# FFN-down of a transformer layer on one core: more 2x2 seven-product panels, with one weight sum formed by transfers

## The chip, the core and the metric

The kernel runs on one core of one Trainium2 chip. The core has five engines with a queue each: PE (TensorE, matrix products; the trace shows its weight loads apart, as PEld), DVE (VectorE), ACT (ScalarE), POOL (GpSimd) and SP (SyncE, which here only issues transfers). Each takes its instructions in order, and semaphores tie the queues together. The metric is the device time of one execution in microseconds (us); of several runs the median is given.

## What is computed

One layer for 256 tokens of width 2048, in float32: RMS norm, an input projection, a pooling mixer and an RWKV-7 mixer, the output projection, then the part that the change touches, and at the end a gate with per-layer embeddings and a final norm:

```python
h2 = rms_norm(x, mlp_norm[i])
x = x + jnp.square(jax.nn.relu(h2 @ w_ffn_up[i])) @ w_ffn_down[i]      # 2048 -> 8192 -> 2048

gate = jax.nn.sigmoid(rms_norm(x, ple_norm[i]) @ w_ple_gate[i])
x = x + gate * (p[i] @ w_ple_proj[i])
```

## The kernel before

**Products.** Each float32 product is made as three products of parts: a value is split into a rounded high part h and the rest l, and h·h, h·l and l·h are summed. A weight panel arrives raw in SBUF (`load_raw`, L149: transfers of 512 KB issued by SP; three buffers with the tag raw and three with raw2). ACT casts it to the high part (wh, two instructions of 512 columns), DVE subtracts to get the low part (wl = raw − wh, one instruction of 1024 columns). Then PE multiplies.

**Stages.** FFN-up and FFN-down run in two halves of 4096 hidden columns. A half is `ffn_half`: eight blocks f of FFN-up (`gemm_wide`; names u00, u01, u10 ... stand for block and half, with four loads each), which leave the activations y, split in h and l; then two sweeps of FFN-down, `down_sweep(hf, pair)`, one for the left and one for the right 1024 output columns. The sweeps are called d00, d01, d10 and d11 (half, then pair). The page and the trace leave numbers out of the names: d_b and d_w are PSUM banks of a sweep, raw_d its raw panels.

**A sweep** runs over 16 panels kp. Each panel is a 256 x 1024 piece of w_ffn_down, taken as a 2x2 of blocks w11, w12, w21, w22 of 128 x 512, against a 2x2 of activation blocks a11 ... a22. A *plain* panel takes the eight block products, each as three matmuls: 24 matmuls. A *square* (in the tuple `SEVEN`) takes seven products (the scheme of Strassen and Winograd): 21 matmuls. For this DVE forms four sums of weight blocks, t1 to t4 (L1269 to L1272), and in FFN-up the sums S of activations (`activation_sums`). Before, there are 7, 7, 7 and 4 squares in d00, d01, d10 and d11.

**Buffers.** In a square of before the halves are 'wa' (w11, its own tag), b (w21, w22), c (w1, w3) and d (w2, w4), in a plain panel a (w11, w12) and b (w21, w22). `halves_of` (L1233) takes them from three pairs with the tags wh and wl, which all stages share, and d from two buffers with the tag graw, which the kept gate weights (`keep`, called in d11 and in the gate's products) use too. The weight sums lie in a8(1, ...), one slot of the large buffers, each 128x2048. One buffer with the tag junk takes the squares of the norms' statistics (`rms_stat`, L298) and the activation sums on their way.

**What sets the order.** The program is written panel by panel, and a scheduler puts each engine's instructions in an order by priority: splits, weight sums and the adds at a sweep's end stand in `tc.high_priority` blocks, and so move ahead of other work as soon as their buffers allow. Buffers of a tag are handed out in the order of the program. At the end of a sweep's last square, the banks of products 1, 5, 6 and 7 are added into x (`add`, L1249), scaled by s2; those of the other four follow at the sweep's end.

## Time and profile before

| | us |
|---|---|
| runs | 1180.05, 1181.89, 1939.81 |
| median of the three | 1181.89 |
| the profiled execution | 1180.25 |
| its span in the trace | 1178.2 |
| first half of FFN-up | about 378 to 558 |
| sweeps d00, d01 | about 558 to 720 |
| second half of FFN-up | about 720 to 902 |
| sweeps d10, d11 | about 902 to 1070 |
| projection, gate, final norm | about 1070 to 1178 |

The span runs from the first to the last instruction of the profiled execution; 2.05 us lie outside it. One of the three runs took 1939.81 us; the other two differ by 0.16%. In the profile's rows, a row of the timeline has the start, the duration, engine, line and operation, the tile written and those read, and in brackets the idle time ahead of it with what ended it. PE's matmuls overlap one another, so their pace is read from start to start. PE's granted clock is 1.00 in all the stages of the table but the last (0.97).

### The profile page before, as it was taken

What the parts mean: (1) busy time and instruction counts of PE and PEld (TensorE: products, weight loads), DVE (VectorE), ACT (ScalarE), POOL (GpSimd) and SP (SyncE); (2) the same over time, 40 slices, a digit from 0 to 9 for tenths busy, and PEclk for the clock granted to TensorE, in tenths of its full rate; (3) what the DMA queues carried; (4) which work ended last, traced back from release to release, by engine and by line L of the source; (5) the groups of instructions that cost most, each with busy time, mean ns of one, the idle gap of its engine ahead of it and who ended that gap; (6) DMA issues with size and microseconds to landing.
All of it is one profiled execution on the core that took longest, in us unless ns stands there. A gap on an engine that the chain in (4) does not pass through costs nothing.

```text
span 1178.2 us, 17287 instructions
## 1 busy us (share of the span) xinstructions
PE 1162.5 (99%) x6419; PEld 973.4 (83%) x6419; DVE 873.3 (74%) x1188; ACT 709.3 (60%) x1309; POOL 13.7 (1%) x73
## 2 busy tenths in 40 slices
PE   8999999999999999999999999999999999999997
PEld 8787777788887888888888888888888888888886
DVE  7786996964656666767988987676668879788543
ACT  7776848676545565555665664555556655568543
POOL 2100000000000000000000000000000000000000
PEclk9999999999999999999999999999999999999999
DMA  7464343354465555555556556555555555767511
GB/s 290 154 202 146 135 140 119 119 179 157 160 203 178 177 182 196 184 192 200 187 204 212 198 202 209 186 191 191 185 195 190 202 205 195 290 233 249 197 56 72
DMA packets 60756, 216.81 MB, mean 184 GB/s; under 512 B 6784, under 2 KB 7552, under 8 KB 60288
## 3 DMA queue, kind: packets, MB, share of 16 engines
q1 hardware_dynamic: 60240, 214.99, 52.5%
q8 instruction: 50, 0.82, 0.3%
q10 hardware_dynamic: 432, 0.73, 0.2%
q14 instruction: 34, 0.28, 0.1%
HBM read 213.59 MB, written 2.10 MB: 183 GB/s over the span
## 4 chain that ended last, share of the span: by engine, by line
PE 96%; ACT 1%; DVE 1%; DMA 0%; issue 0%; SPq 0%; POOL 0%; DVEq 0%; POOLq 0%
PE u_w L1112 20%; PE u_w L1117 10%; PE d_b L1231 7%; PE d_b L1229 7%; PE d_b L1230 7%; PE d_w L1231 2%; PE d_w L1229 2%; PE d_w L1230 2%; PE gt_b L242 2%; PE gt_b L241 2%; PE gt_b L238 2%; PE zk_b L241 1%; PE zk_b L242 1%; PE o_b L241 1%; PE o_b L242 1%; PE zv_b L238 1%
## 5 line engine op out<-in xcount | busy, mean ns | idle before, releaser
L1112 PE MATMUL u_w<-h,wh_u 128*128 128x512 f32 x1024 | 321.9, 395 | 0.0
L167 ACT ACTIVATE wh_u<-raw_u 128x512 fp32r<-128x512 f32 x256 | 147.5, 623 | 160.9 <-issue 98.2
L168 DVE TENSOR_TENSOR wl_u<-raw_u,wh_u 128x1024 fp32r<-128x1024 f32 x128 | 156.6, 1224 | 105.2 <-ACT wh_u L167 103.5
L1117 PEld LDWEIGHTS u_w<-h,wl_u 128*128 128x128 f32 x1024 | 192.4, 188 | 45.4
L1117 PE MATMUL u_w<-h,wl_u 128*128 128x256 f32 x1024 | 201.4, 278 | 0.0
L1112 PEld LDWEIGHTS u_w<-h,wh_u 128*128 128x128 f32 x1024 | 156.0, 189 | 0.1
L168 DVE TENSOR_TENSOR wl_gt<-raw_gt,wh_gt 128x1024 fp32r<-128x1024 f32 x24 | 29.4, 1224 | 23.2 <-ACT wh_gt L167 23.2
L167 ACT ACTIVATE wh_gt<-raw_gt 128x512 fp32r<-128x512 f32 x48 | 28.0, 638 | 23.1 <-PE gt_b L242 14.4
L241 PE MATMUL gt_b<-wh_gt,h 128*128 128x512 f32 x96 | 37.3, 389 | 0.0
L242 PE MATMUL gt_b<-wh_gt,h 128*128 128x512 f32 x96 | 37.3, 389 | 0.0
L168 DVE TENSOR_TENSOR wl_o<-raw_o,wh_o 128x1024 fp32r<-128x1024 f32 x16 | 19.6, 1222 | 12.9 <-ACT wh_o L167 9.9
L167 ACT ACTIVATE wh_o<-raw_o 128x512 fp32r<-128x512 f32 x32 | 18.4, 623 | 16.3 <-issue 8.5
L167 ACT ACTIVATE wh_zp<-raw_zp 128x512 fp32r<-128x512 f32 x32 | 18.6, 623 | 15.7 <-PE zp_b L242 7.2
L168 DVE TENSOR_TENSOR wl_zk<-raw_zk,wh_zk 128x1024 fp32r<-128x1024 f32 x16 | 19.4, 1220 | 10.4 <-ACT wh_zk L167 10.4
L241 PE MATMUL zk_b<-wh_zk,hTh 128*128 128x512 f32 x64 | 25.2, 394 | 1.4 <-ACT wh_zk L167 1.4
L241 PE MATMUL zv_b<-wh_zv,hTh 128*128 128x512 f32 x64 | 26.0, 406 | 0.0
L167 ACT ACTIVATE wh_zk<-raw_zk 128x512 fp32r<-128x512 f32 x32 | 18.4, 622 | 12.4 <-PE zv_b L242 4.0
L241 PE MATMUL zp_b<-wh_zp,hTh 128*128 128x512 f32 x64 | 25.7, 401 | 0.0
L238 PE MATMUL gt_b<-wl_gt,h 128*128 128x512 f32 x96 | 25.7, 389 | 0.0
L168 DVE TENSOR_TENSOR wl_zv<-raw_zv,wh_zv 128x1024 fp32r<-128x1024 f32 x16 | 19.4, 1218 | 8.2 <-ACT wh_zv L167 7.4
L241 PE MATMUL zr_b<-wh_zr,hTh 128*128 128x512 f32 x64 | 25.4, 397 | 0.0
L242 PE MATMUL zp_b<-wh_zp,hTl 128*128 128x512 f32 x64 | 25.0, 391 | 0.0
(840 smaller groups left out, 2963.9 us busy)
## 6 DMA issues: line engine op xcount, KB each, us to landing
raw_u<-in_w_ffn_up_dram SPq DMA_DIRECT2D x128, 512.0 KB, 3.5
raw_d<-in_w_ffn_down_dram SPq DMA_DIRECT2D x128, 512.0 KB, 4.3
raw_gt<-in_w_ple_gate_dram SPq DMA_DIRECT2D x24, 512.0 KB, 3.5
raw_zk<-in_w_in_dram SPq DMA_DIRECT2D x16, 512.0 KB, 3.7
raw_zr<-in_w_in_dram SPq DMA_DIRECT2D x16, 512.0 KB, 3.3
raw_zv<-in_w_in_dram SPq DMA_DIRECT2D x16, 512.0 KB, 3.3
raw_zp<-in_w_in_dram SPq DMA_DIRECT2D x16, 512.0 KB, 3.2
raw_o<-in_w_out_dram SPq DMA_DIRECT2D x16, 512.0 KB, 4.2
```

Of the source, the lines that this page charges most:

```text
L167: nc.scalar.activation(wh[:, a * 512 : (a + 1) * 512], raw[:, a * 512 : (a + 1) * 512], AF.Copy)
L168: nc.vector.tensor_tensor(wl, raw, wh.bitcast(F32), op=ALU.subtract)
L238: nc.tensor.matmul(banks[tt], ah[:, ts_], halves[a][1], start=False, stop=last)
L241: nc.tensor.matmul(banks[tt], ah[:, ts_], halves[a][0], start=i + a == 0, stop=False)
L242: nc.tensor.matmul(banks[tt], al[:, ts_], halves[a][0], start=False, stop=False)
L1112: nc.tensor.matmul(bank[:, ct, :].rearrange("p (s t) -> p s t", s=2), wh[:, cs[ct]], hl, start=k == 0, stop=False, skip_group_check=True,)
L1117: nc.tensor.matmul(bank[:, ct, 0:T], wl[:, cs[ct]], hl[:, 0, :], start=False, stop=k == 15, skip_group_check=True)
L1229: nc.tensor.matmul(banks[n], ah, wh, start=first, stop=False)
L1230: nc.tensor.matmul(banks[n], ah, wl, start=False, stop=False)
L1231: nc.tensor.matmul(banks[n], al, wh, start=False, stop=last)
```

## The change

The layout of w_ffn_down on the host changes, so that a panel's four blocks can be loaded in other groupings. Per square three things change. First, SP loads rx = [w21 | w11] (512 KB) and ry = w22 alone (256 KB). Second, w12 goes into a slot of a *ring* of two slots (one 128x1024 buffer with the tag S) by a transfer that POOL issues, and a second transfer from POOL adds w11 to it on the way, so p1 = w11 + w12 comes without an engine. `begin_sum` issues both; it is called twice in FFN-up (f = 3 and 4), and then after each square, for the square two further on. Third, of the weight sums DVE forms t2 = p1 − w22 in place in the ring, and t43, the two sums for the pair d, in place in rx, with one instruction. w2 is split into a buffer with the tag junk; the tag wa is gone.

There are 9, 9, 9 and 5 squares now; in d00, d01 and d10 mostly two squares follow a plain panel. The half buffers of all panels come from four pairs in turn (three with the tags wh and wl, every fourth pair a pair of its own, wh4 and wl4); graw serves the kept gate weights and the ninth square's activation sums. One activation sum changes its sign, and two adds take ns2 = −s2. The squares of the norm n2 use the tag S ahead of the ring. The order of the panels in d01 changes.

```diff
-                junk = fp.tile([128, 1024], F32, tag="junk", bufs=1, name=f"junk_{name}{tt}{hf}")
+                junk = fp.tile([128, 1024], F32, tag="S" if name == "n2" else "junk", bufs=1, name=f"junk_{name}{tt}{hf}")
...
+        nc.vector.tensor_scalar_mul(ns2, s2, -1.0)
...
-    SEVEN = (1, 3, 5, 7, 9, 11, 13)
-    s_slots = (0, 2, 5)
+    SEVEN = (1, 3, 4, 6, 7, 9, 10, 12, 13)
+    s_slots = (0, 2, 5, 1)
+    ns2 = const.tile([128, 2], F32, name="ns2")
...
-        nc.vector.tensor_tensor(s3, a11, a21, op=ALU.subtract)
+        nc.vector.tensor_tensor(s3, a21, a11, op=ALU.subtract)
...
+    ring = []
+    squares_of = {}
+    visits_of = {}
+    for hf in range(2):
+        for pair in range(2):
+            last = hf + pair == 2
+            squares_of[hf, pair] = (1, 3, 6, 9, 12) if last else SEVEN
+            visits_of[hf, pair] = (0, 2, 1, 4, 3, *range(5, 16)) if last else (range(16), (0, 2, 1, 5, 3, 4, 8, 6, 7, 11, 9, 10, 14, 12, 13, 15))[pair]
+    in_line = [(*hp, kp) for hp, visits in visits_of.items() for kp in visits if kp in squares_of[hp]]
+    begun = []
+    turns = []
+
+    def slot(n):
+        return ring[0][:, n % 2 * 512 : n % 2 * 512 + 512]
+
+    def begin_sum():
+
+        n = len(begun)
+        if not ring:
+            ring.append(fp.tile([128, 1024], F32, tag="S", name="ring"))
+        if n < len(in_line):
+            hf, pair, kp = in_line[n]
+            nc.gpsimd.dma_start(slot(n), w_down[pair, hf * 16 + kp, 1, :, 1, :])
+            nc.gpsimd.dma_start(slot(n), w_down[pair, hf * 16 + kp, 0, :, 1, :], accum_op=ALU.add)
+            begun.append(n)
+
+    def summed(*square):
+        return slot(in_line.index(square))
+
+    def down_sweep(hf, pair, ys, sboxes, hooks=(), between=None):
 
         nm = f"d{hf}{pair}"
+        seven, visits = squares_of[hf, pair], visits_of[hf, pair]
...
-        def halves_of(src, name, own=False):
-
-            pool, kw = (fp, dict(bufs=2)) if own else (wp, {})
-            wh = pool.tile([128, 1024], F32R, tag="graw" if own else "wh", name=f"wh_{name}", **kw)
-            wl = pool.tile([128, 1024], F32R, tag="graw" if own else "wl", name=f"wl_{name}", **kw)
+        def half_tiles(name):
+
+            turns.append(name)
+            if len(turns) % 4 == 0:
+                return [fp.tile([128, 1024], F32R, tag=f"{hl}4", name=f"{hl}_{name}") for hl in ("wh", "wl")]
+            return [wp.tile([128, 1024], F32R, tag=hl, name=f"{hl}_{name}") for hl in ("wh", "wl")]
+
+        def halves_of(src, name):
+
+            wh, wl = half_tiles(name)
...
-        for q, kp in enumerate(((0, 2, 1, 4, 3, *range(5, 16)) if hf else (0, 2, 1, 4, 3, 6, 5, 8, 7, 10, 9, 12, 11, 14, 13, 15)) if pair else range(16)):
+        def add(tt, c, src, scale=s2):
+            nc.vector.scalar_tensor_tensor(xs(tt, c), src, scale[:, tt : tt + 1], xs(tt, c), op0=ALU.mult, op1=ALU.add)
+
+        def panel(kp, c, name, rows):
+
+            return load_raw(w_down[pair, hf * 16 + kp, c, :, 0:rows].rearrange("p r n -> p (r n)"), rows * 512, name)
+
+        for q, kp in enumerate(visits):
             if q in hooks:
                 hooks[q]()
             y, j = ys[kp // 2], kp % 2 * 512
             a11, a21, a12, a22 = ((y[:, j + i * 128 : j + i * 128 + 128], y[:, 1024 + j + i * 128 : 1152 + j + i * 128]) for i in range(4))
-            rx, ry = (load_raw(w_down[pair, hf * 32 + 2 * kp + i], 1024, f"{nm}_{kp}_{i}") for i in range(2))
+            rx, ry = (panel(kp, c, f"{nm}_{kp}_{c}", 1 if c and kp in seven else 2) for c in range(2))
             if kp in seven:
-                i = SEVEN.index(kp)
-                st = sboxes[kp][:, i % 2 * 1024 : i % 2 * 1024 + 1024]
+                st = s_of(sboxes, kp)
                 s1, s2_, s3, s4 = ((st[:, c * 128 : c * 128 + 128], st[:, 512 + c * 128 : 640 + c * 128]) for c in range(4))
-                t_ = a8(1, f"t{nm}_{kp}")
-                t1, t3, t2, t4 = (t_[:, c * 512 : c * 512 + 512] for c in range(4))
-                wa = fp.tile([128, 1024], F32R, tag="wa", name=f"wa{nm}_{kp}")
-                w11 = wa[:, 0:512], wa[:, 512:1024]
+                p1 = summed(hf, pair, kp)
+                t2 = p1
+                wa = fp.tile([128, 1024], F32R, tag="junk", bufs=1, name=f"wa{nm}_{kp}")
+                w2 = wa[:, 0:512], wa[:, 512:1024]
+                w21, w11 = halves_of(rx, f"{nm}_{kp}a")
+                wh, wl = half_tiles(f"{nm}_{kp}b")
+                w22, w1 = ((wh[:, c : c + 512], wl[:, c : c + 512]) for c in (0, 512))
                 with tc.high_priority(20000):
-                    split_sb(*w11, rx[:, 0:512])
-                w21, w22 = halves_of(ry, f"{nm}_{kp}b")
-                with tc.high_priority(20000):
-                    nc.vector.tensor_tensor(t1, rx[:, 512:1024], rx[:, 0:512], op=ALU.subtract)
-                    nc.vector.tensor_tensor(t3, ry[:, 512:1024], rx[:, 512:1024], op=ALU.subtract)
-                    nc.vector.tensor_tensor(t2, t3, rx[:, 0:512], op=ALU.add)
-                    nc.vector.tensor_tensor(t4, ry[:, 0:512], t2, op=ALU.subtract)
-                w1, w3 = halves_of(t_[:, 0:1024], f"{nm}_{kp}c")
-                w2, w4 = halves_of(t_[:, 1024:2048], f"{nm}_{kp}d", True)
-                for n, a_, w_ in (("1", a11, w11), ("2", a12, w21), ("3", s4, w22), ("5", s1, w1), ("7", s3, w3), ("6", s2_, w2), ("4", a22, w4)):
+                    split_sb(*w22, ry[:, 0:512])
+                    split_sb(*w1, p1)
+                    nc.vector.tensor_tensor(t2, p1, ry[:, 0:512], op=ALU.subtract)
+                    t43 = rx.rearrange("p (r n) -> p r n", r=2)
+                    nc.vector.tensor_tensor(t43, t43, t2.unsqueeze(1).to_broadcast([128, 2, 512]), op=ALU.subtract)
+                    split_sb(*w2, t2)
+                w4, w3 = halves_of(rx, f"{nm}_{kp}d")
+                for n, a_, w_ in (("1", a11, w11), ("2", a12, w21), ("3", s4, w22), ("5", s1, w1), ("6", s2_, w2), ("4", a22, w4), ("7", s3, w3)):
                     prod(n, a_, w_)
+                begin_sum()
             else:
-                w11, w12 = halves_of(rx, f"{nm}_{kp}a")
-                for n, a_, w_ in (("2", a11, w11), ("4", a21, w11), ("3", a11, w12), ("x", a21, w12)):
+                w21, w11 = halves_of(rx, f"{nm}_{kp}a")
+                for n, a_, w_ in (("2", a12, w21), ("4", a22, w21), ("2", a11, w11), ("4", a21, w11)):
                     prod(n, a_, w_)
-                w21, w22 = halves_of(ry, f"{nm}_{kp}b")
-                for n, a_, w_ in (("2", a12, w21), ("4", a22, w21), ("3", a12, w22), ("x", a22, w22)):
+                w22, w12 = halves_of(ry, f"{nm}_{kp}b")
+                for n, a_, w_ in (("3", a12, w22), ("x", a22, w22), ("3", a11, w12), ("x", a21, w12)):
                     prod(n, a_, w_)
...
-                    add(0, 1, u)
+                    add(0, 1, u, ns2)
                     nc.vector.tensor_tensor(u, b7, u, op=ALU.add)
                 add(1, 0, u)
-                add(1, 1, u)
+                add(1, 1, u, ns2)
...
+            if f in (3, 4):
+                begin_sum()
...
-        "w_ffn_down": a["w_ffn_down"][0].reshape(64, 128, 2, 1024).transpose(2, 0, 1, 3),
+        "w_ffn_down": a["w_ffn_down"][0].reshape(32, 2, 128, 2, 2, 512)[:, ::-1].transpose(3, 0, 4, 2, 1, 5),
```

The instructions move as follows. In the rows, the first words are the line and the operation, then the tile written and the tiles read. First DVE in the middle of d00, where the weight sums are formed. Before, from panel 8 (plain) to the sums of square 11; 'td' holds the weight sums:

```order
L1241 TENSOR_TENSOR wl_d00_8a_5762<-raw_d00_8_0_5757,wh_d00_8a_5761 128x1024
L173 TENSOR_TENSOR wad00_9_5800<-raw_d00_9_0_5795,wad00_9_5800 128x512
L1241 TENSOR_TENSOR wl_d00_8b_5779<-raw_d00_8_1_5759,wh_d00_8b_5778 128x1024
L1272 TENSOR_TENSOR td00_9_5799<-raw_d00_9_1_5797,td00_9_5799 128x512
L1241 TENSOR_TENSOR wl_d00_9b_5804<-raw_d00_9_1_5797,wh_d00_9b_5803 128x1024
L1241 TENSOR_TENSOR wl_d00_9d_5818<-td00_9_5799,wh_d00_9d_5817 128x1024
L1241 TENSOR_TENSOR wl_d00_9c_5813<-td00_9_5799,wh_d00_9c_5812 128x1024
L1269 TENSOR_TENSOR td00_11_5885<-raw_d00_11_0_5881 128x512
L1270 TENSOR_TENSOR td00_11_5885<-raw_d00_11_1_5883,raw_d00_11_0_5881 128x512
```

After, from square 6 to square 7:

```order
L173 TENSOR_TENSOR wl_d00_6b_5704<-raw_d00_6_1_5695,wh_d00_6b_5703 128x512
L173 TENSOR_TENSOR wl_d00_6b_5704<-ring_4598,wh_d00_6b_5703 128x512
L1316 TENSOR_TENSOR ring_4598<-ring_4598,raw_d00_6_1_5695 128x512
L1318 TENSOR_TENSOR raw_d00_6_0_5693<-raw_d00_6_0_5693,ring_4598 128x1024
L173 TENSOR_TENSOR wad00_6_5697<-ring_4598,wad00_6_5697 128x512
L1283 TENSOR_TENSOR wl_d00_6d_5714<-raw_d00_6_0_5693,wh_d00_6d_5713 128x1024
L1283 TENSOR_TENSOR wl_d00_7a_5747<-raw_d00_7_0_5741,wh_d00_7a_5746 128x1024
L173 TENSOR_TENSOR wl_d00_7b_5752<-raw_d00_7_1_5743,wh_d00_7b_5751 128x512
L173 TENSOR_TENSOR wl_d00_7b_5752<-ring_4598,wh_d00_7b_5751 128x512
L1316 TENSOR_TENSOR ring_4598<-ring_4598,raw_d00_7_1_5743 128x512
```

Where a plain panel stood between two squares there are now two squares behind one another, with one subtraction (L1318) and the split of w2 (wad) directly ahead of the split of the pair d, which reads what ACT casts from L1318's result.

Next DVE at the end of d00, from the last square's last split to the last plain panels; d00_w0 and d00_w1 are the banks of products 1 and 6, and of 5 and 7. Before:

```order
L1241 TENSOR_TENSOR wl_d00_13d_5990<-td00_13_5971,wh_d00_13d_5989 128x1024
L1241 TENSOR_TENSOR wl_d00_13c_5985<-td00_13_5971,wh_d00_13c_5984 128x1024
L1241 TENSOR_TENSOR wl_d00_14a_6030<-raw_d00_14_0_6025,wh_d00_14a_6029 128x1024
L1241 TENSOR_TENSOR wl_d00_14b_6047<-raw_d00_14_1_6027,wh_d00_14b_6046 128x1024
L1249 SCALAR_TENSOR_TENSOR x0_2724<-d00_w0_5411,s2sq_3748,x0_2724 128x512
L1249 SCALAR_TENSOR_TENSOR x0_2724<-d00_w1_5412,s2sq_3748,x0_2724 128x512
L1289 TENSOR_TENSOR ud00_6015<-d00_w0_5411,ud00_6015 128x512
L1249 SCALAR_TENSOR_TENSOR x1_2725<-d00_w1_5412,s2sq_3748,x1_2725 128x512
L1249 SCALAR_TENSOR_TENSOR x0_2724<-ud00_6015,s2sq_3748,x0_2724 128x512
L1241 TENSOR_TENSOR wl_d00_15a_6068<-raw_d00_15_0_6063,wh_d00_15a_6067 128x1024
```

After:

```order
L1283 TENSOR_TENSOR wl_d00_13d_6030<-raw_d00_13_0_6009,wh_d00_13d_6029 128x1024
L1291 SCALAR_TENSOR_TENSOR x0_2724<-d00_w0_5433,s2sq_3748,x0_2724 128x512
L1283 TENSOR_TENSOR wl_d00_14a_6072<-raw_d00_14_0_6067,wh_d00_14a_6071 128x1024
L1336 TENSOR_TENSOR ud00_6057<-d00_w0_5433,ud00_6057 128x512
L1291 SCALAR_TENSOR_TENSOR x0_2724<-d00_w1_5434,s2sq_3748,x0_2724 128x512
L1291 SCALAR_TENSOR_TENSOR x1_2725<-d00_w1_5434,s2sq_3748,x1_2725 128x512
L1291 SCALAR_TENSOR_TENSOR x0_2724<-ud00_6057,ns2_3749,x0_2724 128x512
L1283 TENSOR_TENSOR wl_d00_14b_6089<-raw_d00_14_1_6069,wh_d00_14b_6088 128x1024
L1340 TENSOR_TENSOR ud00_6057<-d00_w1_5434,ud00_6057 128x512
L1283 TENSOR_TENSOR wl_d00_15a_6110<-raw_d00_15_0_6105,wh_d00_15a_6109 128x1024
```

wl of 14b stood ahead of the adds into x; now four adds and one sum (ud00) stand ahead of it.

Last ACT at the start of FFN-up, where h2 is made from the transposed x and the panels of u00 and u01 are cast. Before:

```order
L167 ACTIVATE wh_u00_2_3799<-raw_u00_2_3797 128x512 x2
L1140 ACTIVATE h2_3359<-h2t_3731,par_sb_77 128x256 x2
L167 ACTIVATE wh_u00_3_3822<-raw_u00_3_3820 128x512 x2
L1140 ACTIVATE h2_3359<-h2t_3731,par_sb_77 128x256 x2
L167 ACTIVATE wh_u01_0_3852<-raw_u01_0_3850 128x512 x2
L167 ACTIVATE wh_u01_1_3875<-raw_u01_1_3873 128x512 x2
L167 ACTIVATE wh_u01_2_3898<-raw_u01_2_3896 128x512 x2
```

After:

```order
L167 ACTIVATE wh_u00_2_3800<-raw_u00_2_3798 128x512 x2
L298 ACTIVATE junk_n201_4166,s4_n2_4163<-x0_2724 128x1024
L298 ACTIVATE junk_n210_4168,s4_n2_4163<-x1_2725 128x1024
L1140 ACTIVATE h2_3359<-h2t_3731,par_sb_77 128x256
L298 ACTIVATE junk_n211_4170,s4_n2_4163<-x1_2725 128x1024
L167 ACTIVATE wh_u00_3_3823<-raw_u00_3_3821 128x512 x2
L1140 ACTIVATE h2_3359<-h2t_3731,par_sb_77 128x256
L167 ACTIVATE wh_u01_0_3853<-raw_u01_0_3851 128x512 x2
L1140 ACTIVATE h2_3359<-h2t_3731,par_sb_77 128x256 x2
L172 ACTIVATE wh_d00_1b_5483<-ring_4598 128x512
L167 ACTIVATE wh_u01_1_3876<-raw_u01_1_3874 128x512 x2
```

Three squares of the norm n2 (L298) come between, and the cast of the first sum from the ring stands ahead of the casts of u01_1.

22 lines of the change are left out of this document (12 added, 10 removed).

## The prediction

> **What bounds the kernel now.** I read the profile from the outside in: the page's busy table, slices and chain first, then windows cut at the stages that the change touches, then PE's waits there, then single rows of PE, DVE and ACT. The page, its lines of parts 1, 2 and 4:
>
> ```profile
> PE 1162.5 (99%) x6419; PEld 973.4 (83%) x6419; DVE 873.3 (74%) x1188; ACT 709.3 (60%) x1309; POOL 13.7 (1%) x73
> PE   8999999999999999999999999999999999999997
> PE 96%; ACT 1%; DVE 1%; DMA 0%; issue 0%; SPq 0%; POOL 0%; DVEq 0%; POOLq 0%
> ```
>
> PE carries the end. So matmuls taken away are worth their full time only as long as the other engines still arrive first. The windows are, in order: first half of FFN-up; sweeps d00 and d01; second half of FFN-up; sweeps d10 and d11; the rest.
>
> ```profile
> core 0: us, PE busy (x) PEld busy (x) DVE busy (x) ACT busy (x) POOL busy (x), PEclk, DMA share, GB/s
> 378.00:558.00 180.00, 179.44 (x1034) 156.65 (x1034) 124.46 (x159) 99.07 (x180) 0.00 (x0) 1.00 0.55 188
> 557.90:640.00 82.10, 82.10 (x365) 68.00 (x364) 71.15 (x83) 49.66 (x86) 0.00 (x0) 1.00 0.58 202
> 640.00:720.00 80.00, 80.00 (x354) 66.23 (x353) 69.92 (x79) 47.96 (x83) 0.00 (x0) 1.00 0.58 205
> 902.00:985.00 83.00, 83.00 (x368) 68.71 (x367) 73.13 (x84) 50.17 (x88) 0.00 (x0) 1.00 0.55 196
> 985.00:1070.00 85.00, 85.00 (x385) 69.99 (x384) 71.79 (x82) 53.77 (x100) 0.00 (x0) 1.00 0.72 257
> ```
>
> In the sweeps PE is busy for the whole window, but DVE is busy for 84 to 88% of it (71.79 of 85.00; 73.13 of 83.00). That is the margin which the change spends. From 378 to 1066 PE has one wait:
>
> ```profile
> engine line waited for: us in total, times, longest us
> PE h2t L1134 <- DVE x L1071: 0.6, 1, 0.6
> ```
>
> **What the change takes away.** Three rows of PE's timeline in d00: the first matmul of plain panel 0, of square 1 and of plain panel 2.
>
> ```profile
> 557.93 0.40 PE L1229 MATMUL d_b<-wh_d_0a,y 128*128 128x512 f32 x1
> 563.38 0.39 PE L1229 MATMUL d_w<-wad,y 128*128 128x512 f32 x1
> 568.14 0.39 PE L1229 MATMUL d_b<-wh_d_2a,y 128*128 128x512 f32 x1
> ```
>
> A plain panel's 24 matmuls take 563.38 − 557.93 = 5.45 us, a square's 21 take 4.76: 0.227 us each. Squares go from 25 to 32 (9+9+9+5 for 7+7+7+4), so 7 x 3 x 0.227 = **4.76 us** fewer, 0.4% of the time. If nothing else gave way, the end would come 4.76 us earlier.
>
> **What DVE pays.** One period of d00, DVE's timeline (start, duration, tile, gap before):
>
> ```profile
> 602.90 1.23 DVE L1241 TENSOR_TENSOR wl_d_9c<-td,wh_d_9c 128x1024 fp32r<-128x1024 f32 x1 [1.17 <-ACT wh_d_9c L1240]
> 604.16 0.69 DVE L1269 TENSOR_TENSOR td<-raw_d 128x512 f32<-128x512 f32 x1
> 604.77 0.68 DVE L1270 TENSOR_TENSOR td<-raw_d,raw_d 128x512 f32<-128x512 f32 x1
> 605.49 0.69 DVE L1271 TENSOR_TENSOR td<-td,raw_d 128x512 f32<-128x512 f32 x1
> 606.10 1.22 DVE L1241 TENSOR_TENSOR wl_d_10a<-raw_d,wh_d_10a 128x1024 fp32r<-128x1024 f32 x1
> 607.23 0.68 DVE L173 TENSOR_TENSOR wad<-raw_d,wad 128x512 fp32r<-128x512 f32 x1
> ...
> 629.15 1.40 DVE L1249 SCALAR_TENSOR_TENSOR x<-d_w,s2sq,x 128x512 f32<-128x512 f32 x2
> ```
>
> From start to start a subtraction of 512 columns costs 0.61, one that reads the result just written 0.72 (604.77 to 605.49), one of 1024 columns 1.13 (606.10 to 607.23), an add into x about 0.7. The gap of 1.17 is DVE's spare time: it waits for a half buffer that PE holds. ACT casts a pair of 512 columns in 1.15:
>
> ```profile
> 601.72 1.15 ACT L1240 ACTIVATE wh_d_9c<-td 128x512 fp32r<-128x512 f32 x2 [1.59 <-PE d_b L1231]
> ```
>
> A square after the change: w22 0.61, w1 0.72, t2 0.72, the in-place t43 of 1024 columns 1.24 (its result is waited for), then ACT's pair for d with two hops, 1.23 (w2's 0.61 lies inside it, the rest is a bubble), then d 1.13 and a 1.13: 6.78 against 4.76 of PE. (t43 reads one 512-column operand twice, a form that no row shows; its bounds are one row of 1024 columns, 1.22, and two of 512, 1.38. I take the former, as it is one instruction; the latter would add 0.1 a square.) A plain panel costs DVE 2 x 1.13 = 2.26 against 5.45. So far a plain panel and a square took turns: 10.21 of PE, with 1.17 of it spare on DVE. Now there is one plain panel to two squares: DVE 15.82, PE 14.97. In d00 nothing stands in the bubble, and DVE, not PE, sets the pace while this lasts. In d01 and d10 the next plain panel's a stands ahead of the second square's d and fills one bubble: about 15.2 (15.07 to 15.4), a loss of 0.1 to 0.4 per period.
>
> Cover is four pairs of half buffers, so a loss counts only once DVE's lead is spent. d00, with P the time at which PE starts panel 0: panel 3's last pair is that of square 1, free when PE has ended it at P + 10.2, so w22 of 3 is on DVE at P + 11.0. From there to the end of wl of 14b: 5.63 (3 without its a), seven squares of 6.76, three plain panels of 2.26, and 5.7 for the end, where four adds into x, the two u (L1336, L1340: one lies ahead) and 14a now stand ahead of 14b (before, 14b stood ahead of them). That is P + 76.4. PE wants wl of 14b after five plain panels, nine squares and half of 14, P + 73.0. **Stall in d00: 3.4** (0 if the bubbles are filled by ACT working ahead; twice that, 6.8, if each of the nine squares also waits once more for a hop as long as the bubble). d01 and d10: three or four periods of 0.1 to 0.4, 0.8 each (0 to 1.6). d11: five squares in sixteen panels leave DVE far ahead, 0.
>
> **The start of FFN-up.** Three squares of the second norm move there (the L298 rows in ACT's order of after), since their tag is now the one from which the ring is taken, and the cast of the first sum stands ahead of wh of u01_1. ACT's rows of before:
>
> ```profile
> 381.93 1.15 ACT L167 ACTIVATE wh_u<-raw_u 128x512 fp32r<-128x512 f32 x2 [0.54 <-PE u_w L1112]
> 387.96 1.15 ACT L167 ACTIVATE wh_u<-raw_u 128x512 fp32r<-128x512 f32 x2 [1.64 <-issue]
> 390.75 1.15 ACT L167 ACTIVATE wh_u<-raw_u 128x512 fp32r<-128x512 f32 x2 [1.64 <-issue]
> 391.81 0.58 ACT L1312 ACTIVATE r<-u_w 128x512 f32<-128x512 f32 x1
> 433.61 1.05 ACT L298 ACTIVATE junk_n<-x 128x1024 f32<-128x1024 f32 x1
> ```
>
> Panel u00 ends at 391.8 on PE; one load of u01 lasts 390.75 − 387.96 = 2.8, so wl of u01_1 is wanted at 394.5. Back over DVE's 1.22, ACT's 1.15 and the cast of 0.62, the sum must be there at 391.4. Three norm squares of 1.05 and some 0.2 for reading each out put the ring's start at 382.9. The price of the sum comes from the rows of DMAs (KB, median us to landing), for POOL's queue moves nothing before:
>
> ```profile
> raw_d<-in_w_ffn_down_dram SPq DMA_DIRECT2D x128, 512.0 KB, 4.3
> gu<-in_g_up_dram SPq DMA_DIRECT2D x2, 256.0 KB, 4.2
> wa<-in_wa_up_dram SPq DMA_DIRECT2D x2, 256.0 KB, 2.7
> xq<-in_xT_dram SPq DMA_DIRECT2D x1, 256.0 KB, 5.7
> ```
>
> The two DMAs of a sum run one after the other. Bounds for both together: 5.4 (2 x 2.7) and 11.4 (2 x 5.7). I take 8.4, twice the 4.2 which is also what 512 KB of w_ffn_down take: ready at 391.3, in time. With 11.4 it is 394.3 and the stall 2.9. Behind the cast that waits on ACT stand wh of u01_1 and u01_2, for which DVE and then PE wait, so nothing passes it. I count **0.5** (0 to 3), as 8.4 leaves 0.1 and the ends are uneven. On POOL's queue the accumulation waits for its load, and behind it stands the next square's load; one wait each for a square of some 4 us in a period of 7.5 per square, so that queue keeps up.
>
> **Edits with one answer.** The sums' 32 x 256 KB of extra reading add 8.4 MB to 216.8; the DMA shares of 0.55 to 0.58 in d00, d01 and d10 leave room, and so does d11's 0.72, where only five sums are added. SP's queue loses nothing: it issues one half-sized load for each square and skips none. The raw buffer of rx is held longer, through t43 and d, some 4 us (t43 1.24, the cast 1.23, d 1.13); six raw buffers, three panels ahead (15 us), cover that. The sign of s3 with ns2 moves no work but one 128x2 operation. Kept gate weights apart: the same loads, no fewer.
>
> **Sum.** The profiled execution took 1180.25 (1178.2 of span); the median of the three runs is 1181.89, 1.6 above it, of which one run is 1939.81. 1180.25 − 4.76 + 3.4 + 0.8 + 0.8 + 0.5 = **1181.0**. I forecast no change that can be measured; a measurement of this kernel can tell about 2% from none.
>
> **Rivals.** *B, all hidden:* ACT casts d while DVE works on the next panel, no stall is left, and the whole 4.76 us remains: 1175.5. For it: DVE's 84 to 88% before, and four pairs of buffers. Against it: the sum of 15.82 against 14.97, and in d00 the order has nothing between t43 and d but w2.
>
> *C, the sums come late, slower:* a slot of the ring serves every second square. Its turn is one period, 15.8, of which the square holds it 4.4 (ACT's cast of w1 0.6, then w1, t2, t43 and w2 on DVE, 3.3, and hops), so load and accumulation may take 11.4 together. Above that every period grows by the excess, twelve times in d00, d01 and d10. At 8.4 there are 3 us to spare; at 11.4 none. What could reach further is POOL's issue: if it has to wait for two DVE operations of 1.22 at each of the two DMAs, that is 8.4 + 4 x 1.22 = 13.3, 1.9 over, and 12 x 1.9 = 23 on top: 1204. From 13.3 on it is slower by over 2%. Against it: the landings are medians that include a full SP queue.
>
> The Trainium skill, page "SBUF — State Buffer", section "Who interferes with whom", says that a DMA issued by GpSimd writes its descriptors through a port which DVE's fast-mode operations close, and that one of 620 ns alone took some 3100 ns beside such a copy; by that rule C would be likelier. The trace's rows bear on it only in part: 1024 columns take 1.22 us on DVE, and no DMA from POOL stands there to be compared. The page "DMA: Bandwidth & Descriptors", section "Anatomy of one DMA — SWDGE (gpsimd) path", fits such a DMA with 2.0 us and bytes over 436 per ns; by it two of 256 KB would take an estimated 5.2 us, below every bound above, and the start of FFN-up would not stall: 1180.5.
>
> **How the numbers follow.** A, the feeding limits give the gain back (1177.5 to 1186, likeliest 1181.0): 0.50. The sum of 15.82 leaves out what ACT may do ahead, so B: 0.27. C: 0.20, of which 0.12 beyond 13.3 and 0.08 between 11.4 and 13.3 (1182 to 1204). Others: 0.03, among them a gain of more than 4.76. The range 1174.5 to 1192 takes in A, B (and 1 us below it, for the scatter of single executions) and the lower half of C, and leaves out some 0.15. Faster by over 2%: 0.01; slower by over 2%: 0.12; within: 0.87.
>
> **What would show it.** Right: 21 matmuls fewer (x6419 to x6398); in d00 PE waits for DVE's wl at the squares' d and at 14b, 2 to 5 us in all, with gaps on DVE before d that ACT ends; in d11 none. B: PE's waits in the sweeps stay under 1 us. C: waits of DVE and ACT for the ring, 12 or more, and landings of the accumulations above 6 us. Wrong in any case: PE waiting for raw buffers (SP) in the sweeps, or a wait behind the sweeps that this working does not name.

## The result, and the profile after

The changed kernel takes 1187.47 us (median of 5 runs, 1186.88 to 1189.3) against 1181.89 before. The ratio on record is 1.0058 (interval 1.0046 to 1.0070); it is estimated from all runs but the one of 1939.81 us, and so is not the quotient of the two medians (1.0047). The kernel is slower by 0.5 to 0.6%, and that is clear of the scatter. The forecast was 1181.0, no change to be seen; the time lies inside the range of 1174.5 to 1192, but it moved, and upward.

The page of the changed kernel, the lines that answer to those of before:

```profile
span 1185.3 us, 17422 instructions
PE 1165.6 (98%) x6398; PEld 970.0 (82%) x6398; DVE 892.9 (75%) x1219; ACT 718.9 (61%) x1334; POOL 60.0 (5%) x137
PE   9999999999999999999999999999999999999997
```

The 21 matmuls are gone (6419 to 6398), and yet the span is 7.1 us longer. The tenths hide it: a PE that is late by 0.3 us in 15 still reads 9. So I cut both traces at PE's first matmul of each stage. "Output" runs from the first product of the output projection to the first of FFN-up, "last" from d11 to the first product of the gate.

| us | start of output | output | FFN-up 1 | d00 | d01 | FFN-up 2 | d10 | last | rest | span |
|---|---|---|---|---|---|---|---|---|---|---|
| before | 265.7 | 113.0 | 179.2 | 82.3 | 82.3 | 178.3 | 82.3 | 99.2 | 95.8 | 1178.2 |
| after | 267.2 | 112.9 | 181.1 | 84.7 | 83.5 | 178.3 | 82.4 | 99.2 | 95.9 | 1185.3 |

The start of the output projection lies between 264.6 and 267.3 in the fifteen profiles of this study, in no order that goes with the kernels; 1.5 of the 7.1 us are that. The other 5.6 agree with the difference of the medians. Since two squares more take 2 x 3 x 0.227 = 1.36 us off each of d00, d01 and d10 (one more in d11 0.68), the losses are: FFN-up 1.9, d00 3.8, d01 2.6, d10 1.5, last 0.7: 10.4 in all against the 4.76 saved.

The windows after, in order: first half of FFN-up, d00, d01 and d10. The columns are time, busy time and instructions of PE, PEld, DVE, ACT and POOL, PE's granted clock, and the DMA engines' busy share and GB/s:

```profile
core 0: us, PE busy (x) PEld busy (x) DVE busy (x) ACT busy (x) POOL busy (x), PEclk, DMA share, GB/s
380.00:561.00 181.00, 179.59 (x1030) 156.26 (x1031) 125.48 (x167) 98.79 (x178) 3.04 (x4) 1.00 0.57 193
561.30:646.00 84.70, 83.36 (x360) 66.36 (x359) 76.24 (x85) 51.60 (x93) 12.97 (x18) 1.00 0.74 220
645.90:729.00 83.10, 81.83 (x357) 66.18 (x356) 76.31 (x87) 50.86 (x90) 12.90 (x18) 1.00 0.77 226
907.80:990.00 82.20, 81.97 (x359) 66.52 (x358) 77.14 (x87) 52.60 (x94) 12.92 (x18) 1.00 0.77 238
```

In d00 DVE's busy time rose from 71.15 to 76.24 (in 82.1 and 84.7 us), PE has gaps, and the DMA share went from 0.58 to 0.74. PE's waits, from FFN-up to the gate:

```profile
engine line waited for: us in total, times, longest us
PE u_w L1117 <- DVE wl_u L168: 1.0, 1, 1.0
PE d_b L1267 <- DVE wl_d_7d L1283: 0.8, 2, 0.7
PE d_b L1267 <- DVE wl_d_10d L1283: 0.7, 2, 0.5
PE d_b L1267 <- DVE wl_d_14b L1283: 0.7, 1, 0.7
PE h3t L1134 <- DVE h L1141: 0.6, 1, 0.6
```

Three rows name the places forecast, the second square's d and 14b, but all five add up to little more than a third of the loss, for a wait as listed is only part of what PE loses. At 617.05 in d00 the list has 0.24 us; there PE's matmul starts 0.73 behind the one before it and the next one 0.34 behind that, where 0.227 is usual, so 0.6 is lost. Delays of 0.06 us are not listed at all. The last row lies behind the sweeps, in the projection (at 1085.50): PE's transpose of x for the gate waits for DVE's h and starts 0.98 us behind the matmul before it. The kernel before has no such wait. The first row is FFN-up's. There ACT stood at the cast of the first sum (rows of ACT, then of POOL's issues):

```profile
394.22 0.63 ACT L172 ACTIVATE wh_d_1b<-ring 128x512 fp32r<-128x512 f32 x1 [4.80 <-DMA ring<-in_w_ffn_down_dram]
...
384.40 1.27 POOL L1236 DMA_DIRECT2D ring<-in_w_ffn_down_dram  x2 [127.75 <-ACT wh_u L167]
387.84 0.90 POOL L1237 DMA_DIRECT2D ring<-in_w_ffn_down_dram  x1 [2.16 <-DMA ring<-in_w_ffn_down_dram]
```

The load was issued at 384.4, the accumulation at 387.8, and the sum was there at 394.2: 9.8 us, not 8.4.

One square of d00 on DVE, after:

```profile
588.53 0.69 DVE L173 TENSOR_TENSOR wl_d_6b<-raw_d,wh_d_6b 128x512 fp32r<-128x512 f32 x1
589.14 0.69 DVE L173 TENSOR_TENSOR wl_d_6b<-ring,wh_d_6b 128x512 fp32r<-128x512 f32 x1
589.86 0.69 DVE L1316 TENSOR_TENSOR ring<-ring,raw_d 128x512 f32<-128x512 f32 x1
590.58 1.23 DVE L1318 TENSOR_TENSOR raw_d<-raw_d,ring 128x1024 f32<-128x1024 f32 x1
591.73 0.68 DVE L173 TENSOR_TENSOR wad<-ring,wad 128x512 fp32r<-128x512 f32 x1
593.11 1.23 DVE L1283 TENSOR_TENSOR wl_d_6d<-raw_d,wh_d_6d 128x1024 fp32r<-128x1024 f32 x1 [0.70 <-ACT wh_d_6d L1282]
594.25 1.22 DVE L1283 TENSOR_TENSOR wl_d_7a<-raw_d,wh_d_7a 128x1024 fp32r<-128x1024 f32 x1
595.39 0.68 DVE L173 TENSOR_TENSOR wl_d_7b<-raw_d,wh_d_7b 128x512 fp32r<-128x512 f32 x1
```

From w22 of square 6 to w22 of square 7 it is 595.39 − 588.53 = 6.86 us (6.78 forecast), with the gap of 0.70 ahead of d that ACT ends. PE meets the late d of every second square; the period in d00 and, below it, in d10:

```profile
601.16 0.50 PE L1267 MATMUL d_b<-wl_d_7d,y 128*128 128x512 f32 x1 [0.16 <-DVE wl_d_7d L1283]
617.05 0.50 PE L1267 MATMUL d_b<-wl_d_10d,y 128*128 128x512 f32 x1 [0.24 <-DVE wl_d_10d L1283]
...
932.27 0.50 PE L1267 MATMUL d_b<-wl_d_4d,y 128*128 128x512 f32 x1
947.58 0.50 PE L1267 MATMUL d_b<-wl_d_7d,y 128*128 128x512 f32 x1
```

15.9 us in d00 and 15.3 in d10, where the matmuls alone take 15.0.

In d10 and d01 the next plain panel's a stands in the gap of the second square. DVE in d10 (L1318 is t43):

```profile
936.45 1.22 DVE L1318 TENSOR_TENSOR raw_d<-raw_d,ring 128x1024 f32<-128x1024 f32 x1
938.95 1.23 DVE L1283 TENSOR_TENSOR wl_d_6d<-raw_d,wh_d_6d 128x1024 fp32r<-128x1024 f32 x1 [0.68 <-ACT wh_d_6d L1282]
943.37 1.22 DVE L1318 TENSOR_TENSOR raw_d<-raw_d,ring 128x1024 f32<-128x1024 f32 x1
945.16 1.23 DVE L1283 TENSOR_TENSOR wl_d_8a<-raw_d,wh_d_8a 128x1024 fp32r<-128x1024 f32 x1
946.31 1.22 DVE L1283 TENSOR_TENSOR wl_d_7d<-raw_d,wh_d_7d 128x1024 fp32r<-128x1024 f32 x1
954.27 1.23 DVE L1283 TENSOR_TENSOR wl_d_9d<-raw_d,wh_d_9d 128x1024 fp32r<-128x1024 f32 x1 [0.68 <-PE d_b L1268]
```

From 6d to 9d it is 15.32 us, in which DVE stands still once, for 0.68. So DVE's own rows set the period here too, 0.35 us above PE's.

In d01, PE at the second square's d, ACT at the sum for the same square, and POOL's two issues for that sum:

```profile
690.84 0.39 PE L1266 MATMUL d_w<-wh_d_7d,S 128*128 128x512 f32 x1
691.90 0.50 PE L1267 MATMUL d_b<-wl_d_7d,y 128*128 128x512 f32 x1 [0.68 <-DVE wl_d_7d L1283]
...
685.58 0.63 ACT L172 ACTIVATE wh_d_7b<-ring 128x512 fp32r<-128x512 f32 x1 [0.89 <-DMA ring<-in_w_ffn_down_dram]
...
673.94 0.57 POOL L1236 DMA_DIRECT2D ring<-in_w_ffn_down_dram  x1 [2.87 <-DVE wad L173]
680.21 0.86 POOL L1237 DMA_DIRECT2D ring<-in_w_ffn_down_dram  x1 [5.71 <-DMA ring<-in_w_ffn_down_dram]
```

Here the sum itself was late: ACT stood 0.89 us at its cast, and PE 0.68 at the d behind it.

### The profile page after: what moved, and what is told of

It is laid out like the page before. It is cut to its first block, busy times and chain, and to the rows that moved or that the text cites. A ratio compares the mean times of both kernels' runs of the same rounds, so it can differ in the third digit from the quotient of the medians.

```text
span 1185.3 us, 17422 instructions
## 1 busy us (share of the span) xinstructions
PE 1165.6 (98%) x6398; PEld 970.0 (82%) x6398; DVE 892.9 (75%) x1219; ACT 718.9 (61%) x1334; POOL 60.0 (5%) x137
## 5 line engine op out<-in xcount | busy, mean ns | idle before, releaser
L172 ACT ACTIVATE wad<-ring 128x512 fp32r<-128x512 f32 x32 | 20.2, 633 | 57.0 <-DVE ring L1316 41.5
L1236 POOL DMA_DIRECT2D ring<-in_w_ffn_down_dram x32 | 18.3, 573 | 616.0 <-DVE wad L173 312.4
L1318 DVE TENSOR_TENSOR raw_d<-raw_d,ring 128x1024 f32<-128x1024 f32 x32 | 39.2, 1224 | 1.0
L1237 POOL DMA_DIRECT2D ring<-in_w_ffn_down_dram x32 | 27.8, 869 | 110.3 <-DMA ring<-in_w_ffn_down_dram 110.3
```

What stands on the lines that cost most here:

```text
L172: nc.scalar.activation(h_ap, src_ap, AF.Copy)
L1236: nc.gpsimd.dma_start(slot(n), w_down[pair, hf * 16 + kp, 1, :, 1, :])
L1237: nc.gpsimd.dma_start(slot(n), w_down[pair, hf * 16 + kp, 0, :, 1, :], accum_op=ALU.add)
L1318: nc.vector.tensor_tensor(t43, t43, t2.unsqueeze(1).to_broadcast([128, 2, 512]), op=ALU.subtract)
```

## The experiments

Theory F: DVE with ACT behind it sets the pace in the squares. Theory R: the transferred sums come late. The stages of every run's profile, in us (output and last as above), and the time against runs of the kernel before on the same chip (the ratio, again estimated from all runs, can differ from the quotient of the medians by up to 0.002). The stages are those of one profiled run each:

| run | output | FFN-up 1 | d00 | d01 | d10 | last | median | ratio, interval |
|---|---|---|---|---|---|---|---|---|
| e1_norm_tag | 114.7 | 179.2 | 84.6 | 84.0 | 82.4 | 99.0 | 1185.82 | 1.0046 (1.0029 to 1.0063) |
| e2_no_add | 113.1 | 180.1 | 84.6 | 82.8 | 82.4 | 98.9 | 1184.54, one run | |
| e3_seven | 113.0 | 183.9 | 82.3 | 82.4 | 82.3 | 99.3 | 1184.1 | 1.0024 (1.0014 to 1.0034) |
| e4_two_halves | 113.0 | 182.4 | 83.0 | 82.4 | 85.6 | 98.6 | 1186.85 | 1.0053 (1.0038 to 1.0067) |
| e5_three | 114.7 | 179.2 | 82.1 | 82.2 | 83.9 | 98.7 | 1185.13 | 1.0038 (1.0023 to 1.0053) |
| e6_t2_in_ry | 114.9 | 179.2 | 82.6 | 85.0 | 86.5 | 99.2 | 1194.45 | 1.0108 (1.0083 to 1.0134) |
| e7_t2_only | 112.9 | 185.2 | 85.3 | 84.8 | 88.3 | 100.2 | 1199.29 | 1.0145 (1.0122 to 1.0168) |
| e8_no_w22_low | 113.3 | 183.4 | 81.4 | 83.2 | 82.0 | 98.5 | 1183.99, one run | |
| e9_ring4 | 117.4 | 179.2 | 82.0 | 81.9 | 82.0 | 100.1 | 1185.0 | 1.0035 (1.0022 to 1.0048) |
| e10_ring4_t2 | 117.5 | 179.2 | 80.9 | 85.6 | 80.9 | 100.2 | 1184.74 | 1.0034 (1.0021 to 1.0048) |
| e11_ring4_only | 113.0 | 180.9 | 84.6 | 82.7 | 82.4 | 99.6 | 1184.06 | 1.0029 (1.0018 to 1.0040) |
| e12_best | 113.0 | 179.2 | 80.9 | 81.8 | 80.9 | 99.0 | 1177.05 | 0.9973 (0.9964 to 0.9983) |
| e13_own_pair_first | 113.0 | 179.2 | 82.4 | 82.9 | 82.5 | 99.4 | 1181.55 | 1.0018 (1.0007 to 1.0030) |

**e1_norm_tag.**

```diff
-                junk = fp.tile([128, 1024], F32, tag="S" if name == "n2" else "junk", ...
+                junk = fp.tile([128, 1024], F32, tag="junk", ...
```

> Edit: the four squares of the norm n2 take the tag junk again, as before the change; the ring no longer waits for them. Theory F (the feeding engines, DVE with ACT behind it, set the pace in the squares) and theory R (the transferred sums come late) both put the 2.0 us that the first half of FFN-up gained (179.2 to 181.2 us from its first matmul to that of d00) down to the ring's late start: the first sum landed at 394.2 and ACT stood 4.8 us at its cast. Expected: that stage at 179.2 to 179.7, the sweeps as they are (84.6, 83.6, 82.4), the total 1.5 to 2.0 us lower than the changed kernel. If the cast now waits for its sum further ahead in ACT's order, in the output projection, as much is lost there and the total stays.

FFN-up came back to 179.2, and the output projection went from 112.9 to 114.7. The last clause of the expectation is what happened; ACT's row, in the output projection:

```profile
330.27 0.63 ACT L172 ACTIVATE wh_d_1b<-ring 128x512 fp32r<-128x512 f32 x1 [8.06 <-DMA ring<-in_w_ffn_down_dram]
```

The wait moved with the cast, for an idle ACT and a free half buffer let the scheduler put it as far ahead as the ring was taken. The stages show this; the median's 1.6 us gain comes within the runs' spread.

**e2_no_add.**

```diff
-            nc.gpsimd.dma_start(slot(n), w_down[pair, hf * 16 + kp, 0, :, 1, :], accum_op=ALU.add)
```

> Leaves out the accumulating transfer: a slot of the ring holds w12 alone, so the sums w11 + w12 are missing from the products. All else stands. A sum is there some 5 us earlier (6.3 us for the load and 5.4 for the accumulation were measured in d01). Theory R: the losses of 3.7, 2.7 and 1.5 us in d00, d01 and d10 go, these sweeps come to 81 us each, 7 us in all. Theory F: d00 and d10 stay within 0.4 us of 84.6 and 82.4, d01 loses only the two waits of ACT for the ring (0.9 and 0.4 us), 83.6 to about 82.5. Both: the first half of FFN-up comes back to 179.2 to 180.

d00 and d10 stay at 84.6 and 82.4, d01 is 0.7 shorter. R as the cause of d00's and d10's loss falls; of d01's 2.6 it has 0.7.

**e3_seven.**

```diff
-    SEVEN = (1, 3, 4, 6, 7, 9, 10, 12, 13)
+    SEVEN = (1, 3, 5, 7, 9, 11, 13)
...
-            squares_of[hf, pair] = (1, 3, 6, 9, 12) if last else SEVEN
+            squares_of[hf, pair] = (1, 3, 7, 11) if last else SEVEN
```

The panel orders of before go with it.

> Edit: 7, 7, 7 and 4 squares at the places and in the panel order of the kernel before, all else as changed (ring, four pairs of half buffers, two instructions fewer per square on DVE). A plain panel and a square take turns: DVE 2.26 + 6.78 = 9.0 against 10.2 of PE. Theory F: no loss in the sweeps, 82.3 us each as before, so d00 and d01 are 2.3 and 1.3 us shorter than with nine squares although they have more matmuls, and the total is some 3.5 us under the changed kernel, with FFN-up's 2.0 still in it. Theory R: a slot's turn is 20.4 instead of 15.8 us, the sums are in time, and the same total follows; the two are told apart by the other runs.

All three sweeps are back at 82.3, with all else as changed: the new square alone costs nothing. Two squares in a row do, or the ring's shorter turn that comes with them; this run cannot tell these two apart, e2 and e11 can. FFN-up took 183.9; the sum needed 11.1 us there.

**e4_two_halves.**

```diff
-                    t43 = rx.rearrange("p (r n) -> p r n", r=2)
-                    nc.vector.tensor_tensor(t43, t43, t2.unsqueeze(1).to_broadcast([128, 2, 512]), op=ALU.subtract)
+                    for c in (0, 512):
+                        nc.vector.tensor_tensor(rx[:, c : c + 512], rx[:, c : c + 512], t2, op=ALU.subtract)
```

> Edit: the in-place difference of 1024 columns (t43) is taken as two instructions of 512 columns, one behind the other, so that ACT can cast the first half while DVE makes the second. DVE pays about 0.1 us more for the instructions and waits some 0.55 us less ahead of the split of d. Theory F: a square's chain on DVE goes from 6.8 to 6.3 us, a plain panel and two squares from 15.8 to 14.9, against 15.0 of PE: d00 comes from 84.6 to 81 to 82 us, d01 and d10 gain less (their second square has another split in that gap), 0.3 to 1 us each; total 3 to 5 us under the changed kernel. Theory R: no change within 0.5 us, or slower, since the slot is held as long.

d00 fell to 83.0 and d01 to 82.4, less than hoped, and d10 rose to 85.6. There one sum came late, and PE with it (ACT's waits, d10):

```profile
ACT wh_d_10b L172 <- DMA ring<-in_w_ffn_down_dram: 3.1, 1, 3.1
```

That sum took 13.4 us from the load's issue to the cast. In d01 and d10 the scheduler also put the second square's d ahead of a again. The runs now spread over 6.7 us, and the total is 0.6 under the changed kernel, not 3 to 5, which is within that spread.

**e5_three.** e1 and e4, and:

```diff
-                with tc.high_priority(20000):
+                with tc.high_priority(20000 if pair else 0):
                     add(0, 0, b1)
```

> Three edits together: the norm's tag as in e1, the two halves of e4, and in d00 and d10 the adds of the banks 1, 5, 6 and 7 into x at normal priority, so that wl of 14b stands ahead of them on DVE. e4 left a stall of 0.8 us at wl of 14b in d00 and none of this kind elsewhere. Theory F: d00 from e4's 83.0 to 82.0 to 82.3, FFN-up's first half at 179.2 as in e1, d01 at 82.4 and d10 between 81.3 and 82.4 if the late sum of e4's d10 (a wait of 3.1 us) was scatter; the total at or a little under the kernel before, 1178 to 1181. Theory R: late sums return in one sweep or another, 1 to 3 us each, and the total stays above the kernel before.

d00 82.1, as forecast; d10 83.9, with a wait of 2.2 us for a sum, and e1's wait in the output projection. The total missed by 4 us, and the runs lie between 1180.67 and 1189.44. The late sums of this one profile are as R had it; that they make the spread of the others is not shown.

**e6_t2_in_ry** (e5 with this edit) and **e7_t2_only** (the changed kernel with it):

```diff
-                t2 = p1
+                t2 = ry[:, 512:1024]
```

> e5 with one more edit: t2 = p1 - w22 is written into the unused half of ry's raw buffer instead of the ring. The ring's slot is free as soon as t2 is made, some 2 us earlier per square, and on DVE's order the next square's t2 moves into the gap ahead of the split of d. Theory F: the chain of a square on DVE falls by another 0.7 us where the gap is left; d00 to about 81.3, d01 and d10 to 81.0 to 81.5. Theory R: the same direction through the slot (turn 15.8 less 2.1 instead of 4.4 us, so 13.7 for load and accumulation against 11.7 measured in d01), no wait for the ring in the sweeps. Both: the total under the kernel before, 1176 to 1178.5.

> The changed kernel with this edit alone: t2 into the unused half of ry's buffer. The first half of FFN-up keeps its cost (181 to 184). Theory F: the gap of 0.6 to 0.7 us ahead of the split of d is filled with the next square's t2, the chain of a square falls from 6.8 to 6.1, a plain panel and two squares from 15.8 to 14.5 against 15.0 of PE: d00 from 84.7 to 81.5 to 82.3 (0.8 for 14b remains), d01 and d10 to 81 to 82. Theory R: only d01's 0.7 and the scatter of single late sums go: d00 and d10 stay at 84.6 and 82.4.

Both missed, and by much. DVE's waits in e7, from d00 to d10:

```profile
DVE raw_d L1316 <- DMA ring<-in_w_ffn_down_dram: 19.1, 12, 5.4
```

With t2 freed from the ring, the scheduler set the next square's t2 ahead of this square's d, where its sum had not yet come; and DVE takes its instructions in order, so all splits behind it waited. The gap was filled with a wait.

**e8_no_w22_low.**

```diff
-                    split_sb(*w22, ry[:, 0:512])
+                    nc.scalar.activation(w22[0], ry[:, 0:512], AF.Copy)
+                    w22 = w22[0], w22[0]
```

> Leaves out the low part of w22: DVE's split of 512 columns per square is gone, and the product that uses it takes the high part in its place (the same 21 matmuls). The in-place t43, the gap and the ring stay. Theory F: DVE has 0.61 less per square, a plain panel and two squares cost 14.6 against 15.0, and the losses of d00 shrink as in e4 or more: d00 from 84.7 to 81.8 to 82.5, d10 from 82.4 to 81.0 to 81.4. Theory R: the slot is held as long, so no change in d00 and d10.

d00 81.4: of the 3.8 us lost there 0.5 are left, with gap, ring and matmuls as they were. F holds for d00. d10 came to 82.0 only, and d01 to 83.2. In both the scheduler put the second square's d ahead of a again, and late sums came besides: ACT waited 2.1 us for square 13's in d01 (13.0 us from issue to cast) and 1.2 in d10, and there PE lost most of what these sweeps lost.

**e9_ring4** (from e5), **e10_ring4_t2** (from e6) and **e11_ring4_only** (from the changed kernel):

```diff
-        return ring[0][:, n % 2 * 512 : n % 2 * 512 + 512]
+        return ring[0][:, n % 4 * 512 : n % 4 * 512 + 512]
...
-            if f in (3, 4):
+            if f in (3, 4, 5, 6):
```

The ring has 128 x 2048 elements, and graw one buffer.

> e5 (norm's tag, two halves, late adds) with a ring of four slots instead of two, so a sum is begun four squares ahead; the room comes from graw, one buffer instead of two. After e8, where less work on DVE took d00's loss from 3.7 to 0.4 us while nothing of the ring changed, both theories stand in part: F sets d00's loss in the changed kernel, R sets the scatter and the loss of whatever is made faster than that (e5's runs lie between 1180.7 and 1189.4). F and R together: a slot's turn is two periods, some 30 us, against 12 for a sum, so no wait for the ring is left in the sweeps; d00 82.1 as in e5, d01 81.2 to 82, d10 81.2 to 82, runs within 3 us of each other, total 1177.5 to 1179.5. F alone (the late sums of e5 hidden anyway): as e5, 1181 to 1185, with the same scatter.

> e6 (e5 with t2 in ry's unused half) with the ring of four slots. In e6 and e7 the next square's t2 moved up in DVE's order into the gap ahead of the split of d, and there waited for its sum (four or five waits of up to 2.3 us in d01) with all of DVE's work behind it. R: with sums four squares ahead that wait is gone and the filled gap counts: d00, d01 and d10 at 81.0 to 81.6, total 1176 to 1178. If t2 there waits for ry's own load instead (two waits, 1.8 us, in e7's d00), the sweeps stay at 82 to 83 and the total at 1179 to 1182.

> The changed kernel with the ring of four slots alone (graw with one buffer). R as the whole cause: d00, d01 and d10 all come to 81 and FFN-up alone keeps its loss. F for the sweeps, R for scatter: d00 stays at 84.4 to 84.7 and d10 at 82.4, d01 comes from 83.5 to 82.4 to 82.8, FFN-up's first half stays at 181 to 184 (four sums begin at once there, so the first may land later still); total 1184 to 1187.

e11 gives the clean division, with DVE's splits in the same order as in the changed kernel: d00 and d10 do not move (84.6, 82.4), d01 is 0.8 shorter. In e9 no wait for the ring is left in the sweeps and all three are at 82.0, but the output projection grew to 117.4: four sums begin there, and ACT waited 9.1 us for the first. In e10 d00 and d10 reach 80.9, which is before less 1.4: no loss. Its d01 is at 85.6, where t2 waited for its own panel, as the expectation had feared (DVE's waits in d01):

```profile
DVE raw_d L1316 <- DMA raw_d<-in_w_ffn_down_dram: 6.0, 4, 2.2
```

The totals missed by 5.5 us (e9, the output projection and 0.9 in the last stage) and 6.7 us (e10, d01 besides).

**e13_own_pair_first** (from the changed kernel), and **e12_best** (e10 with it, and t2 in the ring in d01):

```diff
-            if len(turns) % 4 == 0:
+            if len(turns) % 4 == 1:
...
-                t2 = ry[:, 512:1024]
+                t2 = p1 if (hf, pair) == (0, 1) else ry[:, 512:1024]
```

> The changed kernel with one edit: the own pair of half buffers goes to the first, fifth, ... pair of halves. In ACT's order the cast of the first sum leaves the start of FFN-up for its end; the norm's squares, the ring of two slots and the sweeps stay. If FFN-up's loss is the cast that waits for the sum: first half of FFN-up from 181.1 to 179.2 to 180.1 (the upper end if the norm's three squares cost what e2 left there), and the stage ahead as before; sweeps 84.7, 83.5, 82.4 within 0.5 us. If it is the norm's squares or the transfers as such: FFN-up stays at 181 or more.

> e10 with two edits: the pair of half buffers of its own goes to the first, fifth, ... pair of halves instead of the fourth, eighth, ..., so the cast of the first sum has no free buffer early and moves from the output projection (where it held ACT for 8 to 9 us in e1, e5 and e9) to the end of FFN-up; and in d01, where e10's early t2 waited for ry's loads, t2 goes to the ring again. F and R together: the stage from the first product of the output projection to FFN-up as before the change, FFN-up 179.2, d00 and d10 80.9 as in e10, d01 81.9 as in e9, the rest 99.2 to 100.2: 1.4 + 0.4 + 1.4 less and up to 1.0 more than the kernel before, so 1177.5 to 1179.5 against 1180.9, and faster than before by 0.1 to 0.3%. If it is not, what the sweeps gain is given back in a place that these runs have not shown.

e13: FFN-up 179.2 and the output projection 113.0, with the norm's squares and the ring's start left where the change put them. So FFN-up's loss was the place of the cast. d00 fell to 82.4, which was not expected: the other turn of the buffers also made the scheduler put 5a ahead of 4d on DVE, as the changed kernel has it in d10, and d00 then took what d10 takes there. In FFN-up and d00 only the wait that the kernel before has too is listed for PE:

```profile
engine line waited for: us in total, times, longest us
PE h2t L1134 <- DVE x L1071: 0.6, 1, 0.6
```

e12 takes 1177.05 us, 0.27% under the kernel before (0.17 to 0.36), and its ten runs lie within 2.1 us. Every stage came as expected, to 0.1 us, but the last, which did not lose its 1.0, so the total is 0.45 under the range. (Its last stage still has a listed wait of 0.3 us, at d11's first products, for DVE's adds out of the banks.) One square and the next of d00 in e12, on DVE:

```profile
584.88 0.68 DVE L173 TENSOR_TENSOR wl_d_6b<-ring,wh_d_6b 128x512 fp32r<-128x512 f32 x1
585.48 1.28 DVE L1318 TENSOR_TENSOR raw_d<-raw_d,raw_d 128x512 f32<-128x512 f32 x2
586.68 0.68 DVE L173 TENSOR_TENSOR wad<-raw_d,wad 128x512 fp32r<-128x512 f32 x1
587.29 0.68 DVE L1316 TENSOR_TENSOR raw_d<-ring,raw_d 128x512 f32<-128x512 f32 x1
587.89 1.22 DVE L1283 TENSOR_TENSOR wl_d_6d<-raw_d,wh_d_6d 128x1024 fp32r<-128x1024 f32 x1
589.85 1.22 DVE L1283 TENSOR_TENSOR wl_d_7a<-raw_d,wh_d_7a 128x1024 fp32r<-128x1024 f32 x1 [0.75 <-ACT wh_d_7a L1282]
```

The next square's t2 (587.29) stands in the gap without a wait, and d00 has no loss left: 80.9 is the 82.3 of before less 1.36.

## Why the prediction was wrong

DVE as the limit in d00 was right, and nearly so in size. What failed is the rest of the sum: the losses of d01 and d10, of FFN-up's start and of the last stage were put at 0.8, 0.8, 0.5 and nothing, and were 2.6, 1.5, 1.9 and 0.7. All were too small, so they did not cancel, and the gain turned into a loss of 5.6. The time lies above the 1177.5 to 1186 that the forecast gave for its own mechanism; that the stated range holds it is owed to the part added for the rival C, so it is luck. Nor does it take 2% to be told from none, as the forecast had it: 0.6% was enough. Point by point, by its own steps:

- **The saving** of 4.76 us: right. e10 and e12 show it, 80.9 for 82.3 in d00 and d10.
- **DVE sets the pace in d00**: right, in mechanism and nearly in size. 6.86 us per square for 6.78; the period 15.9 for 15.82; stall 3.8 for 3.4. e2 and e11 (nothing but the sums changed: no effect) and e8 (nothing but DVE's work changed: 3.3 us) show that it is this and not the ring. e13 shows what the forecast took as given: it holds for this order of DVE's rows, and a ahead of d takes 2.3 us off.
- **d01 and d10, "0.8 each (0 to 1.6)"**: the step that failed most in the sweeps, by size. The mechanism holds in d10: one gap is filled, DVE's period is 15.3 us (forecast about 15.2), and PE loses 0.33 at the second square's d. That is inside the "0.1 to 0.4" of the working, but near its top, and in all of four periods: 1.3 us, and 0.2 in smaller delays, so 1.5 for 0.8. The filled gap is not free for d: d starts 2.94 us behind t43 (943.37 to 946.31), and 2.50 in the first square, where nothing stands between. d01 was forecast at the same 0.8 with the sums in time; it has d10's loss and 0.7 to 0.8 of late sums besides (e2, e11). The 0.3 that is left there stays open.
- **The start of FFN-up, "I count 0.5 (0 to 3)"**: right place, mis-sized. The sum took 9.8 us for the 8.4 of the working (11.1 in e3), inside its bounds of 5.4 and 11.4, and the stage grew by 1.9. e13 shows that it is the cast's place in ACT's order.
- **C, the sums come late**: nearly right, with less to spare than the working had. d01's late sum took 685.58 − 673.94 = 11.6 us from the load's issue to ACT's cast, of which ACT waited 0.89, so 10.8 would have been in time and not the 11.4 of the budget. The three other late sums of the sweeps say 10.7 to 10.9. These four sums, taken at 8.4 in the working, took 11.0 to 11.7. In the sweeps of the changed kernel C costs 0.7 to 0.8 us; in e6 and e7, where DVE waits for sums directly, it decides the time.
- **The rest, taken as nothing**: d11 and what follows should have been 0.7 shorter and were not. d11's products did end earlier, 85.4 us after its first for 86.2 before, and the wait for DVE's h at 1085.50 gave it back: 0.98 between two starts. In e4 and e8, which have no such wait, the stage is at 98.6 and 98.5, as it should be. This is the wait behind the sweeps that the prediction named as a sign of its working being wrong.

Of the forecast's sum of losses, 5.5 us, and the measured 10.4, FFN-up's start explains 1.4 of the difference, d01 1.8, d10 0.7, d00 0.4 and the last stage 0.7 (with rounding).

By the Trainium skill, page "SBUF — State Buffer", section "Who interferes with whom", POOL's transfers would stand still while a fast-mode operation holds DVE. The same section says that two-operand instructions such as DVE's subtractions in the sweeps (`tensor_tensor`) have no such mode and were not seen to stall a transfer, so the rule, read in full, does not make C likelier, as the prediction had it. The trace agrees: DVE was at work for 76 of 85 us in d00, and POOL's issues there took 0.56 to 0.58 us each for a load and 0.86 to 0.89 for an accumulation, none longer. What the rule says of fast-mode operations no run here shows.

## What to carry to other kernels

When the critical engine is given less to do, write down per period what each feeding engine then has to do, in the order in which its queue has it, and multiply a loss of a third of a microsecond by all the periods that have it. The order counts: one row ahead of another was worth 2.3 us in d00. An instruction that waits for a transfer belongs where the queue has nothing urgent behind it; here the scheduler put such a cast or subtraction far ahead, and that cost 1.7 us in e5's output projection and much more in e7. And cut a trace that is 99% busy at its stages, since a loss of 0.3 us per 15 does not show in tenths.
